# A decoder layer on one core: x and first weights issued in a loop of their own with a fourth raw buffer, constants in a pool that follows the start stage

## The chip, the cores and the metric

The kernel runs on one core of a Trainium2 chip. The metric is the device time of one execution in microseconds (us), as a median over several runs. The engines are named as in the profile: PE is TensorE (matmuls; PEld are its weight loads), DVE is VectorE, ACT is ScalarE, POOL is GpSimd, and SP is SyncE, which in this kernel issues the DMA transfers. GB/s and KB are as the profile prints them.

## The reference

One decoder layer over 256 tokens with 16 learned meta tokens in front (112 inert padding slots ahead of them are not computed by the kernel, so it works on T = 272 tokens). Cut to what matters:

```python
u = rmsnorm(h, attn_norm[l]) * vmask
proj = u @ w_in[l]                       # 2048 -> 6144
aq, ak, av, rq, rk, rv, rg = jnp.split(proj, SPLITS, axis=-1)
lam = jnp.exp(jnp.sum(lq[0] * lq[1])) - jnp.exp(jnp.sum(lq[2] * lq[3])) + lam_init
ya = diff_attention(aq, ak, av, lam, slopes, valid)      # 8 heads, ALiBi bias
ya = rmsnorm(ya, attn_subln[l]) * (1.0 - lam_init)
yr = retention(rq, rk, rv, log_g)                        # 4 heads
yr = rmsnorm(yr, ret_norm[l]) * jax.nn.silu(rg)
h = h + jnp.concatenate([ya, yr], axis=-1) @ w_out[l]
u = rmsnorm(h, ffn_norm[l]) * vmask
h = h + conv_glu(u, w_gate[l], w_up[l], conv_w[l], w_down[l])   # hidden size 5632
out = rmsnorm(h, final_norm)
```

All inputs are float32. The shapes after the arrows and the comments are added here.

## The kernel before

**Matmuls.** Every large product is made of three matmuls per tile of 128x128 weights, with operands split into a high and a low part: high x high, low activations x high weights, high activations x low weights. The weights come from memory in chunks of 128x2048 float32 (1 MB), the tiles `raw0`, `raw1`, ... of pool `wts`, of which there are three buffers. Each chunk is prepared in two halves of 128x1024. ACT casts a half to the high part (`whi`, line 99 in the general loop, line 182 in the start stage), and DVE subtracts it from the chunk to get the low part (`wlo`, lines 100 and 183). `whi` and `wlo` have three buffers each, so the half with number n can be cast only when PE has read half n-3 for the last time, and a chunk's raw buffer comes free when the DVE has made both low parts. Halves are numbered through: chunk c gives `whi` 2c and 2c+1.

**The start stage** (lines 154 to 208). x and four chunks `w_first` are loaded. Here the loop over c = 0..3 runs over the contraction (four of the 16 blocks of 128 rows of x each), and four output tiles (numbers 0 to 3 of the in-projection, `mm0` to `mm3`) are accumulated side by side, by lines 190 to 192, 48 matmuls for each c. The loads of c stand at the head of its body (lines 165 and 166), cut into (0,1), (1,2), (2,4) for c = 0, into two for c = 1, into one for c = 2 and 3. The tile `raw3` is the fourth chunk and takes the buffer of `raw0`. In the same body, `xhi` (ACT, line 174) and `xlo` (DVE, line 175) are the split of x, and the squares for the first norm are taken (lines 195 to 198). Lines 202 to 208 sum them, with one matmul by `ones` (line 205), and make `rstd1` by an inverse square root on DVE (line 127 is the last of its three steps, L125 to L127 in a loop of three). The tiles of this stage lie in a pool `start`, which is closed after it.

**Constants** (lines 210 to 224). lambda_qk (`lq`), the identity, the ALiBi table (`c_alibi`, 86x816), `c_attn_subln`, `c_ret_norm`, `c_ffn_norm` and `c_conv_w` are loaded into the pool `const`, which lives through the kernel. `lam_task` (DVE lines 228 to 234, ACT line 231) makes lambda of `lq`, and `sub8` of `c_attn_subln`. The bias of head 0 is `c_alibi` times a slope (ACT, line 298).

**After the start stage** `gemm` (lines 239 and following) computes the other output tiles one by one, each of one chunk, 48 matmuls by lines 262 to 264. The number `idx` counts output tiles; idx 4 uses halves 8 and 9, idx 5 halves 10 and 11, and so on. idx 4, 5 and 6 are k and v of head 1 (272 wide) and q of head 2 (258 wide); idx 7 uses halves 14 and 15. Attention and retention are put in between as tasks, then come the out-projection and the gated FFN.

**Order.** The order of the program on each engine is not that of the text: a scheduler moves instructions within each engine's stream, and each engine then executes its stream in order. SP issues nearly all loads, in its stream's order, and an issue whose buffer is not free holds up what stands behind it.

Of the kernel before, what the change touches and what calls it, by code (L numbers as in the profile page):

```python
# [10 lines left out]
F32 = mybir.dt.float32  # L11
# [3 lines left out]
AF = mybir.ActivationFunctionType  # L15
# [4 lines left out]
P = 128  # L20
D = 2048
# [3 lines left out]
T = META + SEQ  # L25
# [28 lines left out]
def trunk_kernel(ctx, tc, a, out):  # L54
    nc = tc.nc
    V, S, PE = nc.vector, nc.scalar, nc.tensor

    cp = ctx.enter_context(tc.tile_pool(name="const", bufs=1))
    big = ctx.enter_context(tc.tile_pool(name="big", bufs=1))
    wp = ctx.enter_context(tc.tile_pool(name="wts", bufs=1))  # L60
# [19 lines left out]
    raw = {}  # L80
# [24 lines left out]
    def ahead(hf):  # L105
        while state["dma"] < len(chunks) and state["dma"] <= (hf + 4) // 2:
            load(state["dma"])
            state["dma"] += 1
        while state["prep"] < 2 * len(chunks) and state["prep"] <= hf + 2:
            prep(state["prep"])  # L110
            state["prep"] += 1

    def rsqrt(x, shape, pool, tag, o=None, tags=None):
        tags = tags or (tag + "i", tag + "t", tag + "o")
        i = pool.tile(shape, I32, tag=tags[0], name=tag + "i")
        V.tensor_scalar(out=i, in0=x.bitcast(I32), scalar1=1, scalar2=None,
                        op0=ALU.logical_shift_right)
        V.tensor_scalar(out=i, in0=i, scalar1=-1, scalar2=0x5F3759DF,
                        op0=ALU.mult, op1=ALU.add)
        y = i.bitcast(F32)  # L120
        t = pool.tile(shape, F32, tag=tags[1], name=tag + "t")
        if o is None:
            o = pool.tile(shape, F32, tag=tags[2], name=tag + "o")
        for it in range(3):
            V.scalar_tensor_tensor(out=t, in0=y, scalar=-0.5, in1=x, op0=ALU.mult, op1=ALU.mult)  # L125
            V.tensor_tensor(out=t, in0=t, in1=y, op=ALU.mult)
            V.scalar_tensor_tensor(out=o, in0=t, scalar=1.5, in1=y, op0=ALU.add, op1=ALU.mult)  # L127
            y = o
        return o
# [27 lines left out]
    FN = [(Q0, NQ), (0, T), (0, T), (Q0, NQ)]  # L157
    with tc.tile_pool(name="start", bufs=2) as st:
        acc = st.tile([P, 4, T], F32, name="acc", bufs=1)
        for c in range(4):  # L160
            xr = st.tile([P, 4, T + 1], F32, tag="xr", bufs=4, name=f"xr{c}")
            rw = wp.tile([P, D], F32, tag="raw", bufs=3, name=f"raw{c}")
            cuts = [(0, 1), (1, 2), (2, 4)] if c == 0 else [(0, 2), (2, 4)] if c == 1 else [(0, 4)]
            for b, e in cuts:
                nc.sync.dma_start(out=xr[:, b:e], in_=a["x"][:, 4 * c + b:4 * c + e])
                nc.sync.dma_start(out=rw[:, b * 512:e * 512], in_=a["w_first"][c][:, b * 512:e * 512])
            for half in range(2):
                whi = wp.tile([P, 1024], F32R, tag="whi", bufs=3, name=f"whi{2 * c + half}")
                wlo = wp.tile([P, 1024], F32R, tag="wlo", bufs=3, name=f"wlo{2 * c + half}")
                for jj in range(2):  # L170
                    j = 2 * half + jj
                    k = 4 * c + j
                    xg = xr[:, j, T:T + 1]
                    S.activation(out=xhi[:, k], in_=xr[:, j, :T], func=AF.Copy, scale=xg)
                    V.scalar_tensor_tensor(out=xlo[:, k], in0=xr[:, j, :T], scalar=xg,
                                           in1=xhi[:, k].bitcast(F32),
                                           op0=ALU.mult, op1=ALU.subtract)
                    if c == 0 or jj == 0:
                        n = 512 if c == 0 else 1024
                        d = slice(jj * 512, jj * 512 + n)  # L180
                        src = rw[:, j * 512:j * 512 + n]
                        S.copy(out=whi[:, d], in_=src)
                        V.tensor_tensor(out=wlo[:, d], in0=src, in1=whi[:, d].bitcast(F32),
                                        op=ALU.subtract)
                    for t, (t0, n) in enumerate(FN):
                        b = jj * 512 + t * P
                        wh, wl = whi[:, b:b + P], wlo[:, b:b + P]
                        xh, xl = xhi[:, k, t0:t0 + n], xlo[:, k, t0:t0 + n]
                        o = first[t][:, :n]
                        PE.matmul(o, wh, xh, start=(k == 0), stop=False)  # L190
                        PE.matmul(o, wh, xl, start=False, stop=False)
                        PE.matmul(o, wl, xh, start=False, stop=(k == KT - 1))
            if c == 0:
                S.activation(out=acc, in_=xr[:, :, :T], func=AF.Square)
            else:
                sq = st.tile([P, 4, T], F32, tag="sq", name=f"sq{c}")
                S.activation(out=sq, in_=xr[:, :, :T], func=AF.Square)
                V.tensor_tensor(out=acc, in0=acc, in1=sq, op=ALU.add)
        state["dma"], state["prep"] = 4, 8
        ahead(8)  # L200
        with tc.high_priority():
            V.tensor_tensor(out=acc[:, 0:2], in0=acc[:, 0:2], in1=acc[:, 2:4], op=ALU.add)
            V.tensor_tensor(out=acc[:, 0], in0=acc[:, 0], in1=acc[:, 1], op=ALU.add)
            pst = psx[:, 0]
            PE.matmul(pst[:, :T], ones, acc[:, 0], start=True, stop=True)
            ms = st.tile([P, T], F32, name="ms", bufs=1)
            V.tensor_scalar(out=ms, in0=pst[:, :T], scalar1=EPS, scalar2=None, op0=ALU.add)
            rsqrt(ms, [P, T], st, "r1", rstd1)

    def const(name, shape):  # L210
        t = cp.tile(shape, F32, name="c_" + name)
        nc.sync.dma_start(out=t, in_=a[name])
        return t

    lq = cp.tile([P, 4, 64], F32, name="lq")
    nc.sync.dma_start(out=lq, in_=a["lambda_qk"].unsqueeze(0).to_broadcast([P, 4, 64]))
    idt = const("ident", [P, P])
    base = const("alibi", [QT, 3, T])
    sub = const("attn_subln", [P, 1])
    rn = const("ret_norm", [P, 2])  # L220
    g2 = const("ffn_norm", [P, KT])
# [47 lines left out]
    with ExitStack() as p1:  # L269
# [262 lines left out]
        for j in range(KT):  # L532
            xr = ap_.tile([P, NQ], F32, tag="g0", name=f"xres{j}")
# [6 lines left out]
            else:  # L540
                sq = ap_.tile([P, NQ], F32, tag="rt", bufs=4, name=f"hsq{j}")
# [21 lines left out]
    with ExitStack() as p2:  # L563
# [4 lines left out]
        for f in range(NF):  # L568
# [3 lines left out]
            c = fw.tile([P, SEQ], F32, tag="c", name=f"fc{f}")  # L572
# [152 lines left out]
def build(arrs):  # L725
    import concourse.bacc as _bacc
    import concourse.tile as _tile
    from concourse import mybir as _mybir

    nc = _bacc.Bacc("TRN2", target_bir_lowering=False, num_devices=1)  # L730
    arrays, args = {}, {}
    for name, v in arrs.items():
        arrays[f"in_{name}_dram"] = v
        args[name] = nc.dram_tensor(f"in_{name}_dram", v.shape, _mybir.dt.from_np(v.dtype),
                                    kind="ExternalInput").ap()
    o = nc.dram_tensor("out_0_dram", (SEQ, D), _mybir.dt.from_np(np.dtype("float32")),
                       kind="ExternalOutput").ap()
    with _tile.TileContext(nc, schedule_with_timeline_sim=True) as tc:
        trunk_kernel(tc, args, o)
    return nc, arrays  # L740
# [8 lines left out]
```

## Time and profile before

| | |
|---|---|
| median of 3 runs | 1217.49 us (1216.55 to 1217.88) |
| span of the profiled execution | 1215.7 us |
| busy in the span: PE, PEld, DVE, ACT | 1196.5, 1135.3, 790.7, 558.3 us |
| DMA | 215.71 MB, mean 177 GB/s |

The profiled span lies 1.8 us below the median of the timed runs. The busy time is an average over the stages; the change touches the first 60 us, so the stage's own rows are to be read. Within a row of the timeline the first number is the start in us from the span's start, the second the time that the instructions took, and in brackets stands the idle time of the engine just before, with what ended it. PEclk is the granted clock of TensorE as a share of full speed.

### The profile page before, as it was taken

The numbers are of one execution on the slowest core, as the hardware profiler recorded it, in microseconds if no ns is written. First come the engines' busy times: TensorE is split into PE (matmuls) and PEld (weight loads), VectorE is DVE, ScalarE is ACT, GpSimd is POOL, SyncE is SP. The second block draws the span as 40 slices with busy tenths as digits, with TensorE's granted clock in tenths as the row PEclk, the third lists the DMA queues.
The fourth block names the chain that finished last, engine by engine and source line by source line (L and its number), as shares of the span: only waits on it lengthen the run. The fifth ranks groups of instructions, "written<-read, shape, count | busy, mean of one in ns | idle before, by whom it ended". The sixth has DMA issues, their size and how long they took to land.

```text
span 1215.7 us, 21284 instructions
## 1 busy us (share of the span) xinstructions
PE 1196.5 (98%) x8811; PEld 1135.3 (93%) x8811; DVE 790.7 (65%) x1423; ACT 558.3 (46%) x865; POOL 0.8 (0%) x5
## 2 busy tenths in 40 slices
PE   7999999999999999999999999999999999999996
PEld 6999999999999999999999999999999988888885
DVE  6877787667786557666666666666666645454544
ACT  6465665544445554444444444444444434343442
POOL 0000000000000000000000000000000000000000
PEclk9999999999999999999999999999999999999998
DMA  8443343444445555554554554554555654555552
GB/s 295 149 168 108 140 142 138 163 165 146 153 164 200 196 191 175 193 188 174 189 193 174 184 198 174 179 197 180 177 195 184 210 202 177 196 185 187 194 180 98
DMA packets 34817, 215.71 MB, mean 177 GB/s; under 512 B 4194, under 2 KB 7882, under 8 KB 9760
## 3 DMA queue, kind: packets, MB, share of 16 engines
q1 hardware_dynamic: 34288, 212.58, 49.8%
q8 instruction: 69, 1.13, 0.4%
q0 software_dynamic: 144, 1.05, 0.3%
q10 hardware_dynamic: 288, 0.72, 0.2%
q14 instruction: 28, 0.23, 0.1%
HBM read 212.24 MB, written 2.10 MB: 176 GB/s over the span
## 4 chain that ended last, share of the span: by engine, by line
PE 95%; DMA 2%; DVE 2%; SPq 0%; ACT 0%; issue 0%; DVEq 0%; ACTq 0%
PE mm L262 23%; PE mm L263 23%; PE mm L264 23%; PE o L608 7%; PE o L609 7%; PE o L610 7%; DMA raw<-in_w_first_dram 1%; PE sc L312 1%; PE po L362 1%; PE sc L310 1%; DMA xr<-in_x_dram 1%; DVE wlo L100 0%; PE pa L350 0%; PE rs L402 0%; PE ph L551 0%
## 5 line engine op out<-in xcount | busy, mean ns | idle before, releaser
L99 ACT CAST whi<-raw 128x1024 fp32r<-128x1024 f32 x381 | 399.7, 1049 | 566.1 <-PE mm L263 309.0
L100 DVE TENSOR_TENSOR wlo<-raw,whi 128x1024 fp32r<-128x1024 f32 x381 | 466.3, 1224 | 280.9 <-ACT whi L99 278.0
L262 PE MATMUL mm<-ghi,whi 128*128 128x258 f32 (+1 forms) x1408 | 396.9, 282 | 0.0
L264 PE MATMUL mm<-ghi,wlo 128*128 128x258 f32 (+1 forms) x1408 | 396.7, 282 | 0.0
L263 PE MATMUL mm<-glo,whi 128*128 128x258 f32 (+1 forms) x1408 | 396.1, 281 | 0.0
L263 PEld LDWEIGHTS mm<-glo,whi 128*128 128x128 f32 x1408 | 266.4, 189 | 0.0
L262 PEld LDWEIGHTS mm<-ghi,whi 128*128 128x128 f32 x1408 | 266.0, 189 | 0.0
L264 PEld LDWEIGHTS mm<-ghi,wlo 128*128 128x128 f32 x1408 | 265.8, 189 | 0.0
L262 PE MATMUL mm<-xhi,whi 128*128 128x272 f32 (+1 forms) x688 | 201.5, 293 | 0.0
L263 PE MATMUL mm<-xlo,whi 128*128 128x272 f32 (+1 forms) x688 | 199.3, 290 | 0.0
L264 PE MATMUL mm<-xhi,wlo 128*128 128x272 f32 (+1 forms) x688 | 197.9, 288 | 0.6 <-DVE wlo L100 0.6
L609 PE MATMUL o<-wlo,fhi 128*128 128x512 f32 x340 | 134.1, 395 | 0.0
L610 PE MATMUL o<-whi,flo 128*128 128x512 f32 x340 | 134.1, 395 | 0.0
L262 PEld LDWEIGHTS mm<-xhi,whi 128*128 128x128 f32 x688 | 129.6, 188 | 1.5
L264 PEld LDWEIGHTS mm<-xhi,wlo 128*128 128x128 f32 x688 | 129.5, 188 | 1.0 <-DVE wlo L100 0.8
L263 PEld LDWEIGHTS mm<-xlo,whi 128*128 128x128 f32 x688 | 129.6, 188 | 0.7
L608 PE MATMUL o<-whi,fhi 128*128 128x512 f32 x340 | 120.8, 395 | 0.0
L609 PEld LDWEIGHTS o<-wlo,fhi 128*128 128x128 f32 x340 | 64.0, 188 | 15.0
L610 PEld LDWEIGHTS o<-whi,flo 128*128 128x128 f32 x340 | 64.1, 188 | 14.9
L608 PEld LDWEIGHTS o<-whi,fhi 128*128 128x128 f32 x340 | 64.0, 188 | 14.9
L262 PE MATMUL mm<-yhi,whi 128*128 128x258 f32 x256 | 73.3, 288 | 0.4 <-ACT whi L99 0.4
L263 PE MATMUL mm<-ylo,whi 128*128 128x258 f32 x256 | 72.4, 284 | 0.0
(226 smaller groups left out, 1071.4 us busy)
## 6 DMA issues: line engine op xcount, KB each, us to landing
raw<-in_w_in_dram SPq DMA_DIRECT2D x44, 1024.0 KB, 4.9
raw<-in_w_gate_dram SPq DMA_DIRECT2D x44, 1024.0 KB, 4.8
raw<-in_w_up_dram SPq DMA_DIRECT2D x44, 1024.0 KB, 4.8
raw<-in_w_down_dram SPq DMA_DIRECT2D x44, 1024.0 KB, 4.8
raw<-in_w_out_dram SPq DMA_DIRECT2D x16, 1024.0 KB, 4.9
xres<-in_x_dram SPq DMA_DIRECT2D x16, 129.0 KB, 3.8
raw<-in_w_first_dram SPq DMA_DIRECT2D x2, 1024.0 KB, 13.9
raw<-in_w_first_dram SPq DMA_DIRECT2D x3, 512.0 KB, 7.3
```

Source lines behind the costliest of these rows:

```text
L99: S.copy(out=hi, in_=src)
L100: V.tensor_tensor(out=lo, in0=src, in1=hi.bitcast(F32), op=ALU.subtract)
L262: PE.matmul(ps[:, :n], wh, xh, start=(k == 0), stop=False)
L263: PE.matmul(ps[:, :n], wh, xl, start=False, stop=False)
L264: PE.matmul(ps[:, :n], wl, xh, start=False, stop=(k == KT - 1))
L310: PE.matmul(ps[:QT, m, :nk], q[:, m, qs], k[0][:, m, :nk], start=True, stop=False)
L312: PE.matmul(ps[:QT, m, :nk], q[hs, m, qs], k[1][hs, :nk], start=False, stop=True)
L362: PE.matmul(ps[:QT, i * P:(i + 1) * P], at[j][:n, i - j], vt[:n, j], start=(j == 0), stop=(j == i))
L608: PE.matmul(po[m], ah, wh, start=(k == 0), stop=False)
L609: PE.matmul(po[m], ah, wl, start=False, stop=False)
L610: PE.matmul(po[m], al, wh, start=False, stop=(k == NF - 1))
```

## The change

The loads of x and of `w_first` are issued for all four c in a loop of their own. c = 0 is cut into four pieces, c = 1, 2 and 3 into two each. `raw3` is a tile of its own in the pool `start`, so there are four raw buffers in the start stage; the other three are as before. The splits and matmuls follow in a second loop, and the squares in a third. The constants (`lq` and those by `const`) are taken from a new pool `const2`, opened after `start` is closed, so that their tiles lie in the room that `start` had. The computation is the same.

```diff
     with tc.tile_pool(name="start", bufs=2) as st:
         acc = st.tile([P, 4, T], F32, name="acc", bufs=1)
+        xrs, rws = [], []
         for c in range(4):
             xr = st.tile([P, 4, T + 1], F32, tag="xr", bufs=4, name=f"xr{c}")
-            rw = wp.tile([P, D], F32, tag="raw", bufs=3, name=f"raw{c}")
-            cuts = [(0, 1), (1, 2), (2, 4)] if c == 0 else [(0, 2), (2, 4)] if c == 1 else [(0, 4)]
+            if c < 3:
+                rw = wp.tile([P, D], F32, tag="raw", bufs=3, name=f"raw{c}")
+            else:
+                rw = st.tile([P, D], F32, name="raw3", bufs=1)
+            cuts = [(b, b + 1) for b in range(4)] if c == 0 else [(0, 2), (2, 4)]
             for b, e in cuts:
                 nc.sync.dma_start(out=xr[:, b:e], in_=a["x"][:, 4 * c + b:4 * c + e])
                 nc.sync.dma_start(out=rw[:, b * 512:e * 512], in_=a["w_first"][c][:, b * 512:e * 512])
+            xrs.append(xr)
+            rws.append(rw)
+        for c in range(4):
+            xr, rw = xrs[c], rws[c]
             for half in range(2):
...
+        for c in range(4):
             if c == 0:
-                S.activation(out=acc, in_=xr[:, :, :T], func=AF.Square)
+                S.activation(out=acc, in_=xrs[c][:, :, :T], func=AF.Square)
             else:
                 sq = st.tile([P, 4, T], F32, tag="sq", name=f"sq{c}")
-                S.activation(out=sq, in_=xr[:, :, :T], func=AF.Square)
+                S.activation(out=sq, in_=xrs[c][:, :, :T], func=AF.Square)
                 V.tensor_tensor(out=acc, in0=acc, in1=sq, op=ALU.add)
...
+    cq = ctx.enter_context(tc.tile_pool(name="const2", bufs=1))
+
     def const(name, shape):
-        t = cp.tile(shape, F32, name="c_" + name)
+        t = cq.tile(shape, F32, name="c_" + name)
         nc.sync.dma_start(out=t, in_=a[name])
         return t
 
-    lq = cp.tile([P, 4, 64], F32, name="lq")
+    lq = cq.tile([P, 4, 64], F32, name="lq")
     nc.sync.dma_start(out=lq, in_=a["lambda_qk"].unsqueeze(0).to_broadcast([P, 4, 64]))
```

The streams below show line, operation, output<-input and the shape; the number behind a name tells tiles of one name apart. The lines are those of the kernel that the stream is of: after the change, L169 and L170 are the loads of x and `w_first`, L223 and L227 those of the constants, L309 is the bias, L245 makes `sub8`, and L505 to L510 are the casts and subtractions of q and k (L494 to L499 before).

SP's stream before, from the last load of x to the first chunk of the general loop:

```order
L165 DMA xr3_323<-in_x_dram 128x1092
L216 DMA lq_431<-in_lambda_qk_dram 128x256
L212 DMA c_ident_433<-in_ident_dram 128x128
L212 DMA c_alibi_435<-in_alibi_dram 86x816
L212 DMA c_attn_subln_437<-in_attn_subln_dram 128x1
L212 DMA c_ret_norm_439<-in_ret_norm_dram 128x2
L166 DMA raw3_324<-in_w_first_dram 128x2048
L212 DMA c_ffn_norm_441<-in_ffn_norm_dram 128x16
L212 DMA c_conv_w_443<-in_conv_w_dram 128x132
L87 DMA raw4_394<-in_w_in_dram 128x2048
```

And after the change, from the last piece of x on, with the semaphores that an issue waits for:

```order
L169 DMA xr3_124<-in_x_dram 128x546 [waits DMAHW2_49]
L170 DMA raw3_125<-in_w_first_dram 128x1024 [waits DMAHW3_49]
L87 DMA raw4_400<-in_w_in_dram 128x2048 [waits DMAHW4_49,DVE_49]
L87 DMA raw5_402<-in_w_in_dram 128x2048 [waits DMAHW5_49,DVE_49]
L87 DMA raw6_404<-in_w_in_dram 128x2048 [waits DMAHW7_49,DMAHW6_49,DVE_49]
L87 DMA raw7_593<-in_w_in_dram 128x2048 [waits DMAHW4_49,DVE_49]
L87 DMA raw8_707<-in_w_in_dram 128x2048 [waits DMAHW5_49,DMAHW0_49,DVE_49]
L227 DMA lq_440<-in_lambda_qk_dram 128x256 [waits DMAHW2_49,DMAHW1_49,DMAHW3_49,DVE_49,PE_49]
L223 DMA c_ident_442<-in_ident_dram 128x128
L223 DMA c_alibi_444<-in_alibi_dram 86x816
L223 DMA c_attn_subln_446<-in_attn_subln_dram 128x1
```

`raw3` now stands with the other first weights and no longer waits for DVE (the release of `raw0`), and the constants stand behind `raw8`. The first of them, `lq`, waits for DVE, for PE and for three transfers. The DVE instruction it waits for is the last one of the first norm (the third execution of L127).

ACT's stream before, around the bias of head 0 (`sq3` are the squares of c = 3, and `whi6` and `whi7` its weights):

```order
L174 ACTIVATE xhi1_68<-xr3_323 128x272 x3
L197 ACTIVATE sq3_391<-xr3_323 128x1088
L298 ACTIVATE bias0_478<-c_alibi_435 86x816
L231 ACTIVATE lam_500<-lam_500 128x2
L182 CAST whi6_327<-raw3_324 128x1024
L182 CAST whi7_359<-raw3_324 128x1024
L99 CAST whi8_400<-raw4_394 128x1024
```

And after (`whi13` is the second half of idx 6, `whi14` and `whi15` are the halves of idx 7):

```order
L99 CAST whi13_647<-raw6_404 128x1024
L99 CAST whi14_709<-raw7_593 128x1024
L505 CAST q2_0_470<-q0_464 64x258
L505 CAST q2_0_470<-q0_464 64x258
L508 CAST k2_0_471<-k0_465 64x272
L508 CAST k2_0_471<-k0_465 64x272
L505 CAST q2_1_684<-q1_490 64x258
L505 CAST q2_1_684<-q1_490 64x258
L309 ACTIVATE bias0_487<-c_alibi_444 86x816
L508 CAST k2_1_685<-k1_491 64x272
L508 CAST k2_1_685<-k1_491 64x272
L99 CAST whi15_744<-raw7_593 128x1024
```

The bias went from a place ahead of `whi6` to a place ahead of two casts of k and of `whi15`.

DVE's stream before, around `sub8`, the scaled `c_attn_subln`:

```order
L228 TENSOR_TENSOR lqp_498<-lq_431 128x128
L183 TENSOR_TENSOR wlo5_289<-raw2_253,whi5_288 128x1024
L175 SCALAR_TENSOR_TENSOR xlo_69<-xr3_323,xhi1_68 128x272 x2
L234 TENSOR_SCALAR sub8_446<-c_attn_subln_437 128x1
L230 TENSOR_REDUCE lam_500<-lqp_498 128x2
L175 SCALAR_TENSOR_TENSOR xlo_69<-xr3_323,xhi1_68 128x272 x2
L198 TENSOR_TENSOR acc_101<-acc_101,sq3_391 128x1088
L232 SCALAR_TENSOR_TENSOR nlam_445<-lam_500 128x1
L183 TENSOR_TENSOR wlo6_328<-raw3_324,whi6_327 128x1024
```

And after (`vt0` are copies of transposed v, `kl` and `q2` low parts of k and q):

```order
L510 TENSOR_TENSOR kl_0_472<-k0_465,k2_0_471 64x272
L241 TENSOR_REDUCE lam_509<-lqp_507 128x2
L510 TENSOR_TENSOR kl_0_472<-k0_465,k2_0_471 64x272
L506 TENSOR_TENSOR q2_1_684<-q1_490,q2_1_684 64x258 x2
L352 COPY vt0_483<-pv0_611 100x128
L353 COPY vt0_483<-pv0_611 86x256
L510 TENSOR_TENSOR kl_1_686<-k1_491,k2_1_685 64x272 x2
L100 TENSOR_TENSOR wlo15_745<-raw7_593,whi15_744 128x1024
```

Three instructions ahead of this piece stands `sub8` (L245), with one subtraction of q and one cast of k between. So `sub8` went from a place ahead of `wlo6` to a place ahead of `wlo15`, with ten instructions and `wlo15` queued behind it.

## Rows read from the trace of the kernel before

**Rows 1.** The page: the span, and busy time of each engine.

```profile
span 1215.7 us, 21284 instructions
PE 1196.5 (98%) x8811; PEld 1135.3 (93%) x8811; DVE 790.7 (65%) x1423; ACT 558.3 (46%) x865; POOL 0.8 (0%) x5
```

**Rows 2.** Busy time by stretches: PE, PEld, DVE, ACT, POOL, granted PEclk, DMA share, GB/s.

```profile
10.05:18.00 7.95, 7.95 (x64) 7.95 (x65) 7.55 (x12) 7.84 (x14) 0.00 (x0) 1.00 1.00 404
30.05:35.05 5.00, 5.00 (x22) 5.00 (x23) 4.46 (x5) 1.95 (x2) 0.00 (x0) 0.50 0.27 80
35.05:60.00 24.95, 24.40 (x196) 24.10 (x195) 21.79 (x41) 11.62 (x16) 0.00 (x0) 1.00 0.45 164
60.00:1195.00 1135.00, 1134.58 (x8401) 1078.88 (x8400) 736.72 (x1310) 520.92 (x807) 0.65 (x1) 1.00 0.50 176
```

**Rows 3.** The waits from 0 to 60 us: total, times, longest, in us.

```profile
PE mm L190 <- ACT whi L182: 6.2, 3, 3.9
PE mm L192 <- DVE wlo L183: 0.8, 1, 0.8
```

**Rows 4.** The timeline of PE: waits, the last of idx 4 and of idx 6.

```profile
10.05 0.39 PE L190 MATMUL mm<-xhi,whi 128*128 128x258 f32 x1 [1.63 <-ACT whi L182]
...
30.05 0.58 PE L190 MATMUL mm<-xhi,whi 128*128 128x258 f32 x1 [3.88 <-ACT whi L182]
...
44.64 0.29 PE L264 MATMUL mm<-xhi,wlo 128*128 128x272 f32 x1
...
56.78 0.28 PE L264 MATMUL psx<-xhi,wlo 128*128 128x258 f32 x1
...
57.86 0.39 PE L264 MATMUL mm<-xhi,wlo 128*128 128x272 f32 x1 [0.55 <-DVE wlo L100]
```

**Rows 5.** The chain of waits, in order of time: start, us, what.

```profile
14.91 13.95 DMA raw<-in_w_first_dram
28.95 1.05 ACT whi L182
```

**Rows 6.** The timeline of SP's queue: the issue of the ALiBi table.

```profile
11.46 0.32 SPq L212 DMA_DIRECT2D c_alibi<-in_alibi_dram  x1
```

**Rows 7.** The timeline of ACT.

```profile
11.46 1.05 ACT L182 CAST whi<-raw 128x1024 fp32r<-128x1024 f32 x1
...
26.40 0.88 ACT L298 ACTIVATE bias<-c_alibi 86x816 f32<-86x816 f32 x1 [3.89 <-DMA c_alibi<-in_alibi_dram]
...
44.84 1.05 ACT L99 CAST whi<-raw 128x1024 fp32r<-128x1024 f32 x1 [1.97 <-PE mm L263]
...
49.68 0.86 ACT L497 CAST k<-k 64x272 fp32r<-64x272 f32 x2
```

**Rows 8.** The timeline of DVE.

```profile
26.58 0.15 DVE L234 TENSOR_SCALAR sub<-c_attn_subln 128x1 f32<-128x1 f32 x1 [3.49 <-DMA c_attn_subln<-in_attn_subln_dram]
26.65 0.28 DVE L230 TENSOR_REDUCE lam<-lqp 128x2 f32<-128x128 f32 x1
...
45.93 1.23 DVE L100 TENSOR_TENSOR wlo<-raw,whi 128x1024 fp32r<-128x1024 f32 x1
47.08 0.43 DVE L127 SCALAR_TENSOR_TENSOR rstd<-r1t,rstd 128x272 f32<-128x272 f32 x1
...
49.38 0.61 DVE L498 CAST k<-k 64x272 fp32r<-64x272 f32 x2
...
54.14 0.44 DVE L487 TENSOR_TENSOR v<-mm,rstd 128x272 f32<-128x272 f32 x1
```

**Rows 9.** Busy time from `wlo13`'s end to `wlo14`'s start: columns as in rows 2.

```profile
51.25:56.58 5.33, 5.33 (x47) 5.33 (x47) 5.09 (x14) 3.10 (x5) 0.00 (x0) 1.00 0.57 201
```

**Rows 10.** The timeline of SP's queue: a later load of 86 rows.

```profile
280.93 0.27 SPq L387 DMA_DIRECT2D dk<-in_decay_dram  x1
```

**Rows 11.** Busy time by stretches while that load alone moves: columns as in rows 2.

```profile
283.50:284.00 0.50, 0.50 (x7) 0.50 (x6) 0.50 (x2) 0.33 (x1) 0.00 (x0) 1.00 0.14 47
```

**Rows 12.** The page, DMA issues: KB each, median us from issue to landing.

```profile
raw<-in_w_in_dram SPq DMA_DIRECT2D x44, 1024.0 KB, 4.9
```

## The prediction

> **What bounds the kernel now.** I read the page first, for what limits the whole. PE is busy for 1196.5 of 1215.7 us [rows 1]. The stretches say where the rest is: from 60 to 1195 us PE has 1134.58 of 1135 us, so nothing that comes earlier is caught up later, and each microsecond by which PE reaches 60 us sooner or later is one of the whole time [rows 2]. So only the first 60 us count, and there the list of waits and PE's timeline show four waits that matter: 1.63 us ahead of 10.05, 0.8 us for a low part of weights, 3.88 us ahead of 30.05, and 0.55 us ahead of 57.86 [rows 3, 4]. The longest is followed back by the chain: PE waits for the cast of `whi6` (28.95, 1.05 us), that for `raw3`, issued at 14.91 and landed 13.95 us later [rows 5]. The wait costs more than its length. In the stretch behind it, 30.05 to 35.05, the granted clock is 0.50, the level of 1.2 GHz, and 22 matmuls take 5.00 us, 0.227 each; from 35.05 on it is 1.00 (2.4 GHz), and 196 take 24.40 us, 0.1245 each. So this stretch cost 22 x 0.103 = 2.3 us more [rows 2].
>
> **First weights sent ahead.** Without its wait c = 3 starts at 30.05 - 3.88 - 0.8 = 25.4, if `whi6` is cast by then, so if the first half of `raw3` is there by 24.3. Up to its last piece there are x, four times 128x1092 float32 (0.56 MB), and four chunks of 1.05 MB, together 6.4 MB. While the queue was full it moved 404 GB/s [rows 2], which makes 16 us for all of it, so with some 2 us of lead (below) and a slower start all is there near 20. It would have to come at under 290 GB/s to be late. I take the 3.88 us as gone, the slow clock behind it as gone too, and the 0.8 us as gone since chunk 2 now comes in halves (bound: it stays). Together -3.9 - 2.3 - 0.8 = **-7.0**.
>
> The smaller pieces of c = 0 act on the wait of 1.63 ahead of 10.05. They could give up to 1.6, and I take **0**: ACT casts the first half of c = 1 from 11.46 to 12.5 [rows 7], PE begins with c = 1 right behind that, and as many bytes stand ahead of that half as before. What c = 0 gains is waited for there. Six more issues lie on SP's queue, which waits for free lanes anyway; the squares in a third loop are the same instructions off PE's path. Both 0.
>
> The wait of 0.55 ahead of 57.86 is for `wlo14`, which stood behind all the work on q, k and v of heads 0 and 1. After the change it stands ahead of most of it: **-0.55**.
>
> **Constants later.** Their issues now wait for the last user of the start pool, which is the third L127 of the first norm. When is that? The last matmul of idx 4 started at 44.64 [rows 4], so it ends PE's idx 4 at 44.8 before and 37.8 after the -7.0. `whi12` is cast behind it (1.05; before at 44.84, released by PE [rows 7]), then `wlo12` takes 1.23 [rows 8]: 40.1. In the order of after the change four steps of the norm stand behind `wlo12`, where before only the last did, each about 0.43 plus a gap of 0.03 [rows 8]: the norm ends at 42.0. `lq`, the identity and the ALiBi table are issued one after another, about 0.4 each, so `c_alibi` goes at 42.85.
>
> When does it land? Its 86x816 float32 are 281 kB. The trace of before shows it only from issue at 11.46 to use at 26.40 [rows 6, 7], 14.9 us, in a queue full of weights. A load of 86 rows that moves nearly alone is in the trace later: issued at 280.93 [rows 10], it goes at 47 GB/s and a DMA share of 0.14, about 2 of 16 engines [rows 11]. Its 86x258 float32, 88.8 kB, take 1.9 us at that rate, and the next transfer of weights covers its end at about 284.9, so the lead is about 2.0. At some 46 GB/s 281 kB take 6.1 us: landing at 42.85 + 2.0 + 6.1 = 51.0, and 51.2 with a little sharing with `raw8`. The bounds: 47.7, if it took what a chunk of 1 MB does (4.9 [rows 12]), and 57.8, if 14.9 again. I take 51.2, since the queue carries 164 GB/s in that stretch, 404 in the earlier one [rows 2].
>
> The Trainium skill, page "DMA: Bandwidth & Descriptors", section "Why a DMA increments its semaphore by 16 and not by 1", says that a transfer uses the largest number of engines up to 16 that divides its slowest dimension: for 86 rows, 2. The share of 0.14 agrees with that. Its section "Where 436 GB/s comes from" gives 435.2 GB/s for 16 ports; two of them would be 54.4 GB/s, an estimate by that page, 281 kB in 5.2 us, landing 0.9 earlier and a sum lower by 0.9. The row has 47, so the sum goes by the row.
>
> What waits for it? On ACT the bias stands ahead of two casts of k and `whi15`: 0.88 + 0.86 + 1.05 [rows 7] from 51.2 gives `whi15` at 54.0. On DVE `sub8` waits for `c_attn_subln`, which was issued right behind the table and in before came with it (uses at 26.58 and 26.40 [rows 7, 8]). From `sub8` on, eleven more rows go ahead of `wlo15`. Thirteen like them took 5.09 before [rows 9]; without one q (some 0.43), one k cast (0.30) and one v (0.44), with `sub8` (0.15) and the sum for lambda (0.28) [rows 8] that is 4.35, with gaps 4.5. So `wlo15` starts at 55.8 and ends at 57.0.
>
> When does PE need them? From idx 4's end to idx 6's last matmul 56.78 - 44.64 = 12.1 [rows 4], so idx 6 ends at 49.9, and the first half of idx 7, 24 matmuls, at 52.9. Then it waits 1.1 for `whi15`, can do about four matmuls (0.5), and waits for `wlo15` until 57.0: idle for 57.0 - 52.9 - 0.5 = **+3.6**. Each microsecond of landing is one of this wait; it is zero for a landing at 47.6, so the bounds are about 0 (47.7) and 10.2 (57.8).
>
> **The clock behind that wait.** A wait of 3.88 went with a clock of 0.50 that cost 2.3; behind 1.63 the stretch from 10.05 on shows 1.00 [rows 2, 4]. The new idle time comes in two parts, 1.1 and 2.5, the longer one between those two. I take half, **+1.2**; bounds 0 and 2.3.
>
> **The sum.** -7.0 + 0 - 0.55 + 3.6 + 1.2 = -2.75. The terms are of an execution with a span of 1215.7; the median lies 1.8 above it and I carry the same difference over: 1217.49 - 2.75 = **1214.7**.
>
> **The rivals.**
>
> *The wait for the constants is milder.* With the same landing and no fall of the clock the sum is -4.0; with a landing one microsecond earlier too, -5.0: 1212.5 to 1213.5. For it: the idle time is split by four matmuls. Against: 2.5 is well above 1.63.
>
> *The constants are hidden.* A landing by 47.7 leaves -7.4: 1210.1. Against it speaks the rate of 47 GB/s on 86 rows, which a 1 MB chunk on all engines does not have.
>
> *The table is later and the clock falls fully.* A landing at 53.5 gives a wait of 5.9 and 2.3 for the clock: -7.55 + 8.2 = +0.6, 1218.1.
>
> *Slower.* If the table needs 14.9 us from issue to use as before, it lands at 57.8; the wait is 10.2, the clock 2.3, the sum +5.0: 1222.4. It is slower by over 0.2% from a landing at about 55.1 on, with the full cost of the clock. For it: the only time of this very load. Against: that queue was full.
>
> *The change does not do what it says.* If `raw3` is still as late as before, the 6.2 of the wait and its clock stay and the constants add a wait behind them: -0.8 - 0.55 + 4.8 = +3.4, 1220.9. It needs a rate under 290 GB/s over the first 22 us.
>
> **How the numbers follow.** A difference under 0.2%, 2.4 us, counts as none. The forecast with its own range of -1 to -3.5 has 0.49, the milder wait (-3.5 to -5.2) 0.24, the hidden constants (down to -7.4) 0.08, the later table with -1 to +2.4 0.12, slower by the table 0.05 and by `raw3` 0.02. Faster by over 0.2% are the second and third and some 0.2 of the first: 0.52; slower 0.07; within 0.2% the rest, 0.41. The range from -6 to +0.5, 1211.5 to 1218.0, leaves out most of the hidden constants, half of the later table and the slower cases, under 2 in 10.
>
> **What the profile after would show.** Right: no wait near 25, PEclk 1.00 from 25 to 50, the end of idx 4 some 7 us earlier; the issue of `lq` near 42; the bias waiting for `c_alibi` until 51, `sub8` with it; PE idle twice between 53 and 57, for `whi15` and `wlo15`. Wrong would make it: a landing of the table far from 51, another last user of the start pool, a clock of 0.50 for long behind the wait, or an idle time ahead of c = 1 that shrinks with the pieces of c = 0.

## The result, and where the time went

The changed kernel takes 1218.74 us (median of 20 runs, 1217.78 to 1219.64), the kernel before 1217.05 (20 runs, 1214.17 to 1217.97). The ratio is 1.0015, with an interval of 1.0009 to 1.0021: 0.15% slower, within the bound of 0.2% but clear of noise, where I had forecast 1214.7 and a range up to 1218.0. The prediction was wrong.

The stretches of the changed kernel, with the columns of [rows 2]:

```profile
5.20:10.05 4.85, 4.85 (x33) 4.45 (x34) 3.36 (x7) 3.53 (x7) 0.00 (x0) 1.00 0.92 304
18.00:25.00 7.00, 7.00 (x59) 7.00 (x59) 7.00 (x11) 6.27 (x9) 0.00 (x0) 1.00 1.04 418
25.00:30.00 5.00, 5.00 (x43) 5.00 (x42) 5.00 (x6) 2.10 (x2) 0.00 (x0) 1.00 0.53 221
...
50.00:55.00 5.00, 2.49 (x20) 2.27 (x19) 1.72 (x6) 1.95 (x4) 0.00 (x0) 1.00 0.20 65
55.00:60.00 5.00, 2.37 (x9) 1.83 (x10) 4.86 (x11) 2.69 (x4) 0.00 (x0) 0.70 0.08 11
60.00:65.00 5.00, 5.00 (x25) 4.69 (x24) 1.78 (x5) 1.02 (x2) 0.00 (x0) 0.62 0.90 357
65.00:1195.00 1130.00, 1129.57 (x8360) 1072.38 (x8359) 734.73 (x1306) 518.84 (x806) 0.65 (x1) 1.00 0.50 176
```

From 5 to 50 us PE is busy throughout at full clock: the waits of [rows 4] and the slow stretch of [rows 2] are gone. Between 50 and 60 it is idle for 5.1 us, and then the clock is low. The timelines of the changed kernel show the chain of it, SP's queue first, then ACT, DVE and PE:

```profile
41.44 0.33 SPq L227 DMA_DIRECT2D lq<-in_lambda_qk_dram  x1
...
42.28 0.32 SPq L223 DMA_DIRECT2D c_alibi<-in_alibi_dram  x1
```

```profile
37.27 1.05 ACT L99 CAST whi<-raw 128x1024 fp32r<-128x1024 f32 x1 [1.98 <-PE mm L274]
...
53.00 0.88 ACT L309 ACTIVATE bias<-c_alibi 86x816 f32<-86x816 f32 x1 [6.14 <-DMA c_alibi<-in_alibi_dram]
```

```profile
53.19 0.15 DVE L245 TENSOR_SCALAR sub<-c_attn_subln 128x1 f32<-128x1 f32 x1 [5.76 <-DMA c_attn_subln<-in_attn_subln_dram]
...
57.53 1.23 DVE L100 TENSOR_TENSOR wlo<-raw,whi 128x1024 fp32r<-128x1024 f32 x1
```

```profile
52.20 0.29 PE L275 MATMUL mm<-xhi,wlo 128*128 128x272 f32 x1
55.75 0.39 PE L273 MATMUL mm<-xhi,whi 128*128 128x272 f32 x1 [3.26 <-ACT whi L99]
...
56.79 0.44 PE L273 MATMUL mm<-xhi,whi 128*128 128x272 f32 x1 [0.53 <-ACT whi L99]
...
58.81 0.60 PE L275 MATMUL mm<-xhi,wlo 128*128 128x272 f32 x1 [1.35 <-DVE wlo L100]
```

`whi12` is cast at 37.27 where it was 44.84 [rows 7], 7.57 earlier, and the matmul of idx 7 that ends its first half stands at 52.20 instead of 60.61, where it was before:

```profile
60.61 0.29 PE L264 MATMUL mm<-xhi,wlo 128*128 128x272 f32 x1
```

Then the table is used at 53.00, and `wlo15`, the cause of the last wait, is ready at 58.8. Matmul for matmul, PE is 8.4 us ahead in the first half of idx 7 and 0.1 ahead at 66 us, in idx 8. The three idle times take 3.26 + 0.53 + 1.35 = 5.1 of that by the brackets, and 6.0 when one counts from the start of a matmul to the start of the next, less the usual step (0.126 us, or 0.227 at the low clock): the first matmul behind an idle time takes longer, too. The low clock takes about 2.2, since 22 matmuls of 272 columns start in its stretch, 0.227 apart instead of 0.126:

```profile
57.00:63.90 6.90, 5.55 (x24) 5.10 (x23) 4.37 (x7) 0.69 (x1) 0.00 (x0) 0.51 0.55 199
```

So at 66 us the two kernels are level. The rest comes from the last stage. Of each kernel one group of its matmuls, with their number, the shortest, median and longest in ns, and the first and last start in us (the number at the end of the row is of a sample), first before, then after:

```profile
L609 PE MATMUL o<-wlo,fhi x340: 390/393/404, 960.6 to 1201.1; 128*128 128x512 f32 x170
```

```profile
L620 PE MATMUL o<-wlo,fhi x340: 392/395/397, 960.4 to 1201.9; 128*128 128x512 f32 x170
```

The changed kernel begins the stage 0.2 us earlier (0.3 us gained in the out-projection, which ends 504 us ahead of it in both kernels) and takes 241.5 instead of 240.5 us for the same matmuls, without a wait in either. The span of the profiled execution is 1216.7 against 1215.7. The medians lie further apart, 1.7 us, partly since the execution of before that was profiled (1217.5) was slower than the median of its 20, and that of after (1218.5) faster than the median of its own.

### The profile page after: what moved, and what is told of

The parts are those of the page before. It is cut to its first block, busy times and chain, and to the rows that moved or that the text cites. A ratio compares the mean times of both kernels' runs of the same rounds, so it can differ in the third digit from the quotient of the medians.

```text
span 1216.7 us, 21296 instructions
## 1 busy us (share of the span) xinstructions
PE 1199.2 (99%) x8811; PEld 1134.7 (93%) x8811; DVE 790.1 (65%) x1423; ACT 557.8 (46%) x865; POOL 0.8 (0%) x5
## 4 chain that ended last, share of the span: by engine, by line
PE 96%; DVE 1%; DMA 1%; ACT 0%; issue 0%; SPq 0%; DVEq 0%; ACTq 0%
PE mm L273 23%; PE mm L274 23%; PE mm L275 23%; PE o L619 7%; PE o L621 7%; PE o L620 7%; PE sc L323 1%; PE po L373 1%; DMA c_attn_subln<-in_attn_subln_dram 1%; PE mm L198 1%; PE mm L200 1%; PE mm L199 1%; PE sc L321 1%; PE pa L361 0%; PE rs L413 0%; DMA raw<-in_w_first_dram 0%
## 5 line engine op out<-in xcount | busy, mean ns | idle before, releaser
L620 PEld LDWEIGHTS o<-wlo,fhi 128*128 128x128 f32 x340 | 63.8, 188 | 15.6
L621 PEld LDWEIGHTS o<-whi,flo 128*128 128x128 f32 x340 | 63.8, 188 | 15.4
L275 PE MATMUL mm<-yhi,wlo 128*128 128x258 f32 x256 | 72.2, 284 | 0.0
```

Of the source, the lines that this page charges most:

```text
L275: PE.matmul(ps[:, :n], wl, xh, start=False, stop=(k == KT - 1))
L620: PE.matmul(po[m], ah, wl, start=False, stop=False)
L621: PE.matmul(po[m], al, wh, start=False, stop=(k == NF - 1))
```

## The experiments

The first four ask which part of the change gains and which loses. **The table in two transfers:**

```diff
+        if name == "alibi":
+            nc.sync.dma_start(out=t[:80], in_=a[name][:80])
+            nc.sync.dma_start(out=t[80:], in_=a[name][80:])
+        else:
+            nc.sync.dma_start(out=t, in_=a[name])
```

> The changed kernel with the ALiBi table loaded in two transfers, of 80 and of 6 rows; all else is as in the changed kernel, the constants still wait for the start pool. First theory: the table is late because its 86 rows go through two engines. Then the 80 rows land near 46, neither the bias nor sub8 is waited for, PE has no idle time between 52 and 59, PEclk is 1.00 there, and the ratio to the kernel before is 0.993 to 0.994 (some 8 us less). Rival: it is late because it is issued late and shares the queue with weights. Then it still lands at 50 or later, a wait of 2 us or more and the slow clock stay, and the ratio is 0.997 or more.

Measured: 1211.28 us, ratio 0.9955 (0.9943 to 0.9968). ACT's and PE's timelines:

```profile
47.22 0.89 ACT L313 ACTIVATE bias<-c_alibi 86x816 f32<-86x816 f32 x1
```

```profile
53.62 0.39 PE L279 MATMUL mm<-xhi,wlo 128*128 128x272 f32 x1 [0.29 <-DVE wlo L100]
```

```profile
50.00:55.00 5.00, 4.71 (x38) 4.49 (x37) 4.89 (x10) 2.02 (x3) 0.00 (x0) 1.00 0.13 23
55.00:60.00 5.00, 5.00 (x39) 4.72 (x38) 3.91 (x12) 1.80 (x5) 0.00 (x0) 1.00 0.94 375
```

The issue is as late as in the changed kernel (42.62), but the bias waits for nothing any more; PE's three idle times are down to one of 0.29, and the clock stays up. So the loss is the table's transfer through few engines, not the late issue by itself. The Trainium skill's page "DMA: Bandwidth & Descriptors", section "Why a DMA increments its semaphore by 16 and not by 1", has a transfer use the largest number of engines, up to 16, that divides its slowest dimension, by which 80 rows go through 16 and 86 through 2. This run, where the wait of 6.14 us for the table is gone, and the run with 43 and 43 rows below (23 to 25 GB/s) agree. The ratio is not as low as the 0.993 to 0.994 expected.

**The constants back in the first pool** (the rest as changed):

```diff
-    cq = ctx.enter_context(tc.tile_pool(name="const2", bufs=1))
...
-        t = cq.tile(shape, F32, name="c_" + name)
+        t = cp.tile(shape, F32, name="c_" + name)
...
-    lq = cq.tile([P, 4, 64], F32, name="lq")
+    lq = cp.tile([P, 4, 64], F32, name="lq")
```

> The changed kernel with the constants back in the first pool, so that they wait for no release of the start pool; they are issued behind raw4. First theory: what the change gains in the start stage is lost only to the constants' wait. Then the wait for whi15 and wlo15 is gone, the table lands near 32, and the ratio is 0.993 to 0.994. Rival: the gain is lost whatever the constants do, since the weights of the general loop are late next: then PE waits for whi9 to whi12 instead and the ratio is 0.997 or more.

Measured: 1210.84 us, ratio 0.995 (0.9938 to 0.9963). The table is issued at 17.25, and PE is idle for under 1 us between 50 and 55:

```profile
45.00:50.00 5.00, 5.00 (x44) 5.00 (x43) 4.87 (x13) 4.37 (x10) 0.00 (x0) 1.00 0.64 215
50.00:55.00 5.00, 4.25 (x34) 4.03 (x33) 4.85 (x11) 2.10 (x2) 0.00 (x0) 1.00 0.00 0
```

**The fourth buffer alone**, in the kernel before:

```diff
-            rw = wp.tile([P, D], F32, tag="raw", bufs=3, name=f"raw{c}")
+            if c < 3:
+                rw = wp.tile([P, D], F32, tag="raw", bufs=3, name=f"raw{c}")
+            else:
+                rw = st.tile([P, D], F32, name="raw3", bufs=1)
```

> The kernel before with the fourth raw buffer alone: cuts, loops and the constants' pool as before. First theory: the wait of 3.88 and its slow clock come from raw3 waiting for raw0's buffer behind the constants. Then raw3 lands near 20, the wait ahead of c = 3 and the clock of 0.50 are gone, and the ratio is 0.994 to 0.995 (6 to 7 us less). Rival: raw3 was late because the constants filled the queue; then a wait of 2 us or more stays there, and the ratio is 0.997 or more.

Measured: 1211.88 us, ratio 0.9957 (0.9944 to 0.9971). PE's waits:

```profile
10.14 0.39 PE L193 MATMUL mm<-xhi,whi 128*128 128x258 f32 x1 [1.51 <-ACT whi L185]
...
21.42 0.75 PE L195 MATMUL mm<-xhi,wlo 128*128 128x258 f32 x4 [0.78 <-DVE wlo L186]
...
33.77 0.39 PE L267 MATMUL mm<-xhi,wlo 128*128 128x272 f32 x1 [0.74 <-DVE wlo L100]
```

The wait of 3.88 is gone, and with it the low clock; the others remain. That of 0.78 is absent in every run with the finer cuts and the loop of the loads (no run parts these two). That at 10 us comes and goes by itself: in two runs below with the order of before it is none (shifted by 32 bytes) and 1.02 (the room alone). Like the first run, the second and third gain some 1 to 2 us less than expected; why is not shown.

**The later constants alone**, in the kernel before (the reverse of the second edit):

> The kernel before with the constants in the later pool alone, three raw buffers and the old cuts. First theory: raw3 still waits for raw0's buffer, but with no constants ahead of it in SP's stream it is issued near 12 and lands near 20, so most of the wait of 3.88 goes; the constants' wait behind the first norm comes in, as in the changed kernel: ratio 1.000 to 1.003. Rival: without the fourth buffer the wait stays, and the new wait comes on top: ratio 1.005 or more.

Measured: 1217.87 us, ratio 1.001 (1.0001 to 1.0019). `raw3` is issued at 11.48 here, and PE has no wait ahead of c = 3. So either remedy, the buffer or an empty queue, frees c = 3. But the new wait is there too, 4.07 us of PE in one piece:

```profile
53.38 0.88 ACT L300 ACTIVATE bias<-c_alibi 86x816 f32<-86x816 f32 x1 [6.46 <-DMA c_alibi<-in_alibi_dram]
```

```profile
54.93 0.60 PE L266 MATMUL mm<-xhi,wlo 128*128 128x272 f32 x1 [4.07 <-DVE wlo L100]
```

In these runs the last stage showed the second loss. The group of L609 above takes 240.5 us with the constants in the first pool (second and third run) and 241.5 with the later pool (first and fourth). What lies where differs: with the constants out of the first pool, all that is allocated behind it, `whi` and `wlo` too, lies 5472 bytes lower in each partition, and starts at 32 mod 64. Two runs shift by 32 bytes.

```diff
+    pad = cp.tile([P, 8], F32, name="pad")
+    V.memset(pad, 0.0)
     warm = cp.tile([P, 512], BF16, name="warm")
```

In the changed kernel:

> The changed kernel with an unused tile of 32 bytes per partition in the first pool; its instructions and their order are those of the changed kernel. In the changed kernel, whi and wlo start at an address that is 32 mod 64, in the kernel before at a multiple of 64; here at a multiple of 64 again. Theory: the 1056 matmuls of the last stage, which stream whi and wlo 512 wide, are slower by their moving operand's address; then the stage takes 245.1 us from its first to its last matmul, as before, instead of 246.2, and the ratio to the kernel before is 1.0005 to 1.001 instead of 1.0015. Rival: it is something else of the later pool (or of the fourth buffer); then it stays 246.2.

In the kernel before:

> The kernel before with the same unused tile of 32 bytes, so that whi and wlo start at 32 mod 64; nothing else differs. Theory of the address: the last stage takes 246.2 us instead of 245.1 and the ratio is 1.0008. Rival: 245.1 and 1.000.

Measured: ratio 1.0011 (1.0002 to 1.002) and 1.0004 (0.9995 to 1.0014). The times can't tell, but the rows can, first the changed kernel shifted, then the kernel before shifted:

```profile
L622 PE MATMUL o<-wlo,fhi x340: 392/396/397, 959.6 to 1201.1; 128*128 128x512 f32 x170
```

```profile
L611 PE MATMUL o<-wlo,fhi x340: 390/393/405, 959.7 to 1200.2; 128*128 128x512 f32 x170
```

241.5 and 240.5, as without the shift. A theory of the address modulo 64 falls.

**Two transfers with the shift**, in the changed kernel:

> The changed kernel with the table in two transfers of 80 and 6 rows and with the unused tile of 32 bytes. Both effects are apart in place, so if both theories hold they add: 1.0 us less than with the two transfers alone, ratio 0.994 to 0.995, under both kernels. Rival for the address: 0.9955 as with the two transfers alone.

Measured: 1210.95 us, ratio 0.9952 (0.994 to 0.9965), the same as the first run within the intervals; its last stage is as slow as there (241.5), as the rival has it.

**The room alone.** The kernel before, with only the pool of the constants opened behind the others at the start. All four engines execute the very order of before, and the operands lie where the changed kernel has them:

```diff
     sp = ctx.enter_context(tc.tile_pool(name="small", bufs=2))
+    cq = ctx.enter_context(tc.tile_pool(name="const2", bufs=1))
...
-        t = cp.tile(shape, F32, name="c_" + name)
+        t = cq.tile(shape, F32, name="c_" + name)
...
-    lq = cp.tile([P, 4, 64], F32, name="lq")
+    lq = cq.tile([P, 4, 64], F32, name="lq")
```

> The kernel before with the pool of the constants opened behind the other pools instead of in the first one: the instructions and their order are those of the kernel before, the constants are loaded as early as there, but x's parts, htok, raw, whi and wlo lie 5472 bytes lower, where the changed kernel has them. The shift by 32 bytes did not change the last stage. Theory: the step of its 1056 matmuls depends on where its operands lie; then the stage takes 246.2 us as in the changed kernel, the 512 matmuls on y take 96.4 instead of 96.7, and the ratio is 1.0005 to 1.001. Rival: it comes of the changed order of the program; then 245.1 and 96.7 stay and the ratio is 1.000.

Measured: ratio 1.0012 (1.0003 to 1.0021), and in the trace:

```profile
L610 PE MATMUL o<-wlo,fhi x340: 392/395/397, 960.4 to 1201.9; 128*128 128x512 f32 x170
```

241.5 us in the order of before. So the last stage's 1.0 us is the place of its operands, not the program's order. All 14 traces agree: the group takes 241.5 us in the nine with the constants in the later room and 240.5 in the five with the first pool. Which operand, and what about its place, stays open.

**The clock behind the wait.** 28 matmuls of zeros between the halves of idx 7:

```diff
+            if idx == 7 and half == 1:
+                for i in range(28):
+                    PE.matmul(ps[:, :n], warm[:, :P], warm[:, :n], start=False, stop=False)
```

> The changed kernel with 28 matmuls of zeros (272 wide, bf16, added to the same sums) between the two halves of idx 7, so that PE works through the first part of the wait for whi15 (3.26 us idle in the changed kernel; 28 take about 3.2). Theory: a part of the loss, about 2.9 us, is the slow clock that follows the idle time. Then PEclk stays 1.00 from 52 to 65 and the ratio to the kernel before is 0.999 instead of 1.0015. Rival: the clock is not tied to this idle time; then the stretch with 0.50 stays and the ratio is 1.0015 or more.

Measured: 1220.05 us, ratio 1.0023 (1.0013 to 1.0034). PE's timeline:

```profile
52.39 3.19 PE L268 MATMUL mm<-warm 128*128 128x272 bf16 x26
...
59.50 0.35 PE L324 MATMUL sc<-k,q 128*86 128x100 f32 x1 [3.92 <-DVE q L496]
```

This run does not decide. The filling moved the idle time instead of closing it: the scheduler put matmuls of scores, which wait for a DVE result behind `wlo15`, ahead of the last zeros, so one idle time of 3.92 stands where three were, and the clock is low behind it as before (0.50 from 60 to 65 us).

**The table, slower still.** The first edit with 43 and 43 rows:

> The changed kernel with the table in two transfers of 43 rows each. Theory: a transfer's engines follow from its rows (two for 86, many for 80 in the earlier run); 43 has no divisor up to 16 but 1, so each half goes through one engine, and if it is the same one the table takes twice as long: it lands at 59 or later instead of 53, the waits of the bias, of whi15 and of wlo15 grow by 6 us or more, and the ratio is 1.006 to 1.008. Rival: two transfers side by side move as fast as one of 86 rows; then it lands near 53 and the ratio is 1.0015.

Measured: 1222.68 us, ratio 1.005 (1.0036 to 1.0064). PE, and the stretches in which the table moves alone:

```profile
60.31 0.59 PE L277 MATMUL mm<-xhi,whi 128*128 128x272 f32 x1 [7.38 <-ACT whi L99]
```

```profile
54.00:56.00 2.00, 0.00 (x0) 0.00 (x0) 0.00 (x0) 0.00 (x0) 0.00 (x0) 1.00 0.08 25
56.00:58.00 2.00, 0.00 (x0) 0.00 (x0) 0.00 (x0) 0.00 (x0) 0.00 (x0) 0.67 0.07 23
```

23 to 25 GB/s at a DMA share of 0.07 to 0.08, about one engine of 16 and half of the 47 GB/s of [rows 11]: both halves go through the same one, as the first theory has it. The bias starts at 58.44, 5.4 later than in the changed kernel; PE's idle time grows by 3.8 (7.38 + 0.22 + 1.30 = 8.9), less than the 6 expected, and the ratio stays below the expected 1.006.

**Both remedies**, the second and the first edit together:

> The changed kernel with the constants in the first pool (as early as raw4) and the table in two transfers of 80 and 6 rows. Theory: both remedies take away the same wait, so together they give little more than each: the first 60 us as with early constants or up to 0.7 us better, since the table no longer holds up weights behind it, and the last stage at 245.1 as in the kernel before; ratio 0.9945 to 0.995. Rival: the weights behind the constants are late; then PE waits 2 us or more between 30 and 55 and the ratio is 0.9965 or more.

Measured: 1209.79 us (1209.37 to 1209.79), ratio 0.9942 (0.9929 to 0.9954), the best of all kernels here. PE has no idle time from 20 to 75 us:

```profile
40.00:50.00 10.00, 10.00 (x84) 10.00 (x84) 9.69 (x22) 7.81 (x13) 0.00 (x0) 1.00 0.40 145
50.00:60.00 10.00, 10.00 (x74) 9.29 (x73) 7.94 (x19) 3.30 (x7) 0.00 (x0) 1.00 0.55 210
```

**The table without the weights beside it.** In the changed kernel the next chunk moves while the table does:

```profile
46.00:48.00 2.00, 2.00 (x19) 2.00 (x18) 1.40 (x3) 0.81 (x2) 0.00 (x0) 1.00 1.02 265
48.00:50.00 2.00, 2.00 (x19) 2.00 (x18) 0.00 (x0) 0.00 (x0) 0.00 (x0) 1.00 1.02 269
```

```diff
     def load(c):
         t = wp.tile([P, D], F32, tag="raw", bufs=3, name=f"raw{c}")
+        if c == 9:
+            nc.sync.dma_start(out=t[:, :16], in_=chunks[c][:, :16])
+            raw[c] = raw[8]
+            state["kept"] = t
+            return
...
+        if hf == 18:
+            V.tensor_copy(out=junk0, in_=state["kept"][:, 0:1])
```

> The changed kernel without the load of weight chunk 9 (1 MB), whose issue stands right behind the constants: 8 KB of it are loaded, the output tile of chunk 9 is made of chunk 8, and one copy of a column on DVE (0.15 us) holds its buffer back, so that no weights move while the table does. Theory: the table landed 1.8 us later than reckoned because chunk 9 moved beside it from 46 to 50.5. Then it is used near 50.4 (issue at 42.3, 2.0 of lead, 281 kB at 46 GB/s) instead of 53.0, PE's wait shrinks from 5.1 to about 2.5, and the ratio to the kernel before is 0.998 to 1.0. Rival: 86 rows of 3264 bytes are slower by themselves, or the lead is longer; then the table is used near 53 and the ratio stays 1.001 to 1.002.

Measured: 1217.05 us, ratio 1.0001 (0.9992 to 1.001). ACT and PE:

```profile
51.74 0.89 ACT L316 ACTIVATE bias<-c_alibi 86x816 f32<-86x816 f32 x1 [4.68 <-DMA c_alibi<-in_alibi_dram]
```

```profile
54.49 0.39 PE L280 MATMUL mm<-xhi,whi 128*128 128x272 f32 x1 [1.80 <-ACT whi L104]
```

The table comes 9.3 us after its issue (42.48) instead of 10.7, between the two expectations. PE is idle for 3.9 us instead of 5.1. Sharing with the chunk is worth some 1.5 us of the landing; another 0.9 beyond my 8.35 (51.2 less 42.85) is there without it. The stretches of this run show where:

```profile
44.00:46.00 2.00, 2.00 (x19) 2.00 (x18) 1.93 (x7) 1.93 (x5) 0.00 (x0) 1.00 0.14 30
...
48.00:50.00 2.00, 2.00 (x19) 2.00 (x18) 0.00 (x0) 0.00 (x0) 0.00 (x0) 1.00 0.16 60
```

By the trace's DMA records, five of the table's 86 rows start by 43.8, none in the next 2.0 us, and the others from 45.9 to 51.1, at some 50 GB/s. So the table moves faster than the 46 GB/s reckoned, but stands still for about 2 us near its start. In the changed kernel it pauses there, too; what holds it up is not shown.

## Why the prediction was wrong

**What bounds the kernel** held: from 97 us to the out-projection the two traces stay within 0.2 us of each other, matmul for matmul.

**First weights sent ahead**, -7.0 and -0.55: right. PE was 7.6 us ahead by idx 4 and 8.4 in the first half of idx 7. That is 0.9 more than the sum, mostly since a wait cost PE 0.2 to 0.3 us beyond its bracket (the 3.88 cost 4.0 and the 0.55 cost 0.8, from start to start). The third run shows the fourth buffer to be enough for the wait of 3.88 and its clock; the 0.8 went with the finer cuts and the loop of the loads. For the pieces of c = 0 I had 0, and almost nothing is what was left of them, but not as I had read it:

```profile
13.10 0.28 PE L190 MATMUL mm<-xhi,whi 128*128 128x258 f32 x1
```

```profile
12.43 0.39 PE L198 MATMUL mm<-xhi,whi 128*128 128x258 f32 x1
```

This is the first matmul of c = 1, before and after. Before, it did not stand right behind its cast, which ended at 12.5: PE was still at c = 0. After, it does, 0.67 earlier, but short stops ahead of the matmuls with the low parts leave 0.13 of that at the start of c = 2 (18.92 instead of 19.05). The transfers do not set that: ACT, which casts all of it, is busy from 7.9 to 24.2 without a wait for a load.

**Constants later**: the mechanism was right step by step (the last norm step, the bias and `sub8` in front of `whi15` and `wlo15`, two engines for the table), the size was not. `lq` went at 41.44 (reckoned 42.05), but the table was used at 53.0, not 51.2. The step that failed is "landing at 42.85 + 2.0 + 6.1 = 51.0, and 51.2 with a little sharing with `raw8`". It was `raw9` that shared, the chunk issued right behind the constants, and the last run measured about 1.5 us for it; I had looked only at what was ahead in the queue. The other 0.9 comes of the table's standstill near its start, less what its faster rate gives back; no term had it, and its cause is open. The term was 5.1 instead of 3.6 by the brackets, and 6.0 from start to start: 1.8 of the 2.4 by the later landing, and 0.6 because PE ended the first half of idx 7 at 52.3 and not at 52.9. The wait for `whi15` was the longer part, 3.26, not the shorter one.

**The clock behind that wait**: 2.2 instead of 1.2, close to my bound of 2.3. I had set half of the old stretch's cost since the idle time came in parts. It cost all of it: from 57.0 to 63.8 the granted clock is 0.50, and as in the stretch of [rows 2] 22 matmuls fall into it. That the cost goes with the wait is shown by the first run, where both are gone; how it depends on the wait's length and parts is not settled, as the run with the zeros moved the wait.

**What no term had**: +1.0 in the last stage and -0.3 in the out-projection, from the place of the operands. I treated the constants' move from one pool to another as a move in time alone. The run with the room alone, with the order of before, shows it to be the room.

Together -8.4 + 6.0 + 2.2 - 0.3 + 1.0 = +0.5, and +1.0 between the spans; the rest is in small differences (0.2 between idx 8 and the out-projection, 0.2 behind the last stage). Of the rivals, "the table is later and the clock falls fully" (+0.6, a chance of 0.12) is the one that came true, 0.5 us before its landing of 53.5. That its sum lies so near is partly luck: the gain ahead of the wait was 0.9 larger than the sum has it, and the room's 0.7 is not in the sum. Without that 0.7 the time would have been 1218.0, at the range's upper end.

## What to carry to other kernels

A constant loaded late costs nothing only if nobody queues behind it: look for what stands behind its first user on ACT and DVE, and for the large transfers issued right behind it as well as ahead. Look at a load's row count: 80 + 6 rows in place of 86 took the whole wait away here, and 43 + 43 made it longer. When tiles move to another pool, compare the matmul step of every later stage too, since all that lies behind it moves.

## What the runs showed of the hardware that was not expected

The same 512-wide matmuls in the same order take 0.4% longer when their operands lie 5472 bytes lower (241.5 against 240.5 us for the group above), while a shift by 32 bytes changes nothing. The out-projection's 258-wide matmuls gain 0.3 of 96.7 us by the same shift of 5472, and those of the stage between, gate and up, take 504.2 us either way.

The low clock behind a wait is not the same in every execution of the same order. Before, the clock fell during the wait, and 30.05 to 35.05 ran at 0.50 throughout [rows 2]; in the run with the room alone, behind a wait of 4.53 that ended at 30.71, it was low only from 31.2 to 34.6, and the stretch reads:

```profile
30.00:35.00 5.00, 4.29 (x22) 4.29 (x23) 4.31 (x5) 2.65 (x3) 0.00 (x0) 0.66 0.21 52
```
